# Attention scores on one core: head-pair weights 128 columns wide, 16 KB store runs, and transposes in groups of sixteen

## The chip, the cores and the metric

The kernel runs on one NeuronCore of a Trainium2 chip. A core has a matrix engine (TensorE, PE in the profile; its weight loads are listed as PEld), three engines for element-wise work (VectorE = DVE, ScalarE = ACT, GpSimd = POOL), a queue engine (SyncE = SP) that issues transfers here, and 16 DMA engines that move data between the device memory and the on-chip memory SBUF. Matmul results land in PSUM, which DVE and ACT can read[...]. The metric is the device time of one execution in microseconds (us). Before the change it is 203.78 us, the median of three runs (203.74 to 204.09).

## The reference

```python
batch, heads, seq, dim = 8, 8, 512, 64
q, k = randn(batch, heads, seq, dim), randn(batch, heads, seq, dim)   # float32
def reference(q, k):
    scale = 1.0 / np.sqrt(q.shape[-1])
    return (np.einsum('bhqd,bhkd->bhqk', q, k) * scale).astype(np.float32)
```

For each of 64 (batch, head) pairs, q (512 x 64) is multiplied with k transposed (64 x 512). The inputs are 16.8 MB, the output is 67.1 MB of float32.

## The kernel before

**Units and tiles.** The work is cut into four units `v`, each of two batches, that is 16 (batch, head) pairs. A unit gives four output tiles `t`, so there are 16 tiles `o`, each 128 partitions x 32 KB = 4 MB, covering four heads. Tiles and their stores are numbered 0 to 15 below.

**Loads and casts.** All loads are issued at the start by SP (line 78): per unit k and q, 2 MB each, into one 4 MB buffer of the pool `big`. GpSimd casts them to bf16 (line 82), in two instructions for each of k and q, into `xb`. The pool `big` has three buffers, which the loads and the output tiles share in turn: the load of unit 3 waits for the casts of unit 0, tile 0 takes the buffer whose casts (unit 1) come next, tile 1 that of unit 2, tile 2 that of unit 3, and from tile 3 on each tile waits for the store three before it.

**Transposes.** A load puts 128 rows of sequence on partitions, with two sets `s` side by side so that a 128 x 128 block holds two 64-wide heads' worth of columns. PE transposes such blocks by a product with the identity (line 107 for k, line 116 for q), eight into one PSUM tile `tp` of one bank; the pool `tpsum` has two of them. Each group of eight is then moved by four copies (line 95) of 64 partitions x 512 columns, one for each set `s` and half `h` of a head pair, into `kT` or `qz`. The four copies of a group are all on one engine; groups alternate between DVE and ACT. A unit has four groups for k and four for q. `qz` is zeroed once and holds, for each head pair, the queries of one head in the rows of that head and zeros in the others, so that a contraction over 128 rows gives a single head's scores.

**Scores.** For an output tile, eight times, four matmuls (line 126) fill a PSUM tile `ps` of two banks (three such tiles in the pool `psum`): each takes 64 weight columns of `qz` and 512 columns of `kT`, and two of them fill the upper and lower 64 partitions of one bank. Then one evacuation of 128 x 1024 float32 scales it into the tile `o`, on ACT (line 64) in turns 0, 2 and 3 of every six and on DVE (line 66) in the others. After eight evacuations SP issues the store of the 4 MB (line 141).

**The order of work.** The program order is kept on each engine. `transpose` is a generator: it yields once after the transposes of a group and once after each copy, so a group is five steps. Unit 0's groups are all run first. Then, while the tiles of unit v are computed, the steps of unit v + 1 are put between the evacuations by `take` (line 162): for v = 0 none in tile 0 and two after each evacuation from tile 1 on, later one after each evacuation and two after every fourth. Each engine works through its instructions in that order.

Of the kernel before, what the change touches and what calls it, by code (L numbers as in the profile page):

```python
# [1 line left out]

# [5 lines left out]


@with_exitstack  # L10
def kernel(
    ctx: ExitStack,
    tc: tile.TileContext,
    q: bass.AP,
    k: bass.AP,
    out: bass.AP,
):

    nc = tc.nc
    B, H, S, D = q.shape
    scale = 1.0 / (D ** 0.5)
    P = 128
    UNITS = B // 2
    N = H
    M = P // (2 * H)  # L30
    R = S // M
    J = R // 2
    RO = 16
    U = S // RO
    JJ = J // RO
    IW = 8 // JJ
    TILES = N // 2

    f32 = mybir.dt.float32
    bf16 = mybir.dt.bfloat16  # L40

    q_r = q.rearrange("(v b) g (m j) d -> v (b g m) (j d)", b=2, j=R)
    k_r = k.rearrange("(v b) g (m j) d -> v (b g m) (j d)", b=2, j=R)
    out_r = out.rearrange("(v b) (t h) (u i) k -> v (b t) (h u) (i k)", b=2, h=4, i=RO)

    consts = ctx.enter_context(tc.tile_pool(name="consts", bufs=1))

    big_pool = ctx.enter_context(tc.tile_pool(name="big", bufs=3))
    bf_pool = ctx.enter_context(tc.tile_pool(name="bf", bufs=6))
    t_pool = ctx.enter_context(tc.tile_pool(name="t", bufs=2))  # L50
    tpsum_pool = ctx.enter_context(tc.tile_pool(name="tpsum", bufs=2, space=bass.MemoryType.PSUM))
    psum_pool = ctx.enter_context(tc.tile_pool(name="psum", bufs=3, space=bass.MemoryType.PSUM))


    pinned = tc.keep_in_program_order

    n_evac = 0
    n_tp = 0

    def evacuate(dst, src):  # L60
        nonlocal n_evac

        if n_evac % 6 in (0, 2, 3):
            pinned(nc.scalar.mul(out=dst, in_=src, mul=scale))  # L64
        else:
            pinned(nc.vector.tensor_scalar(out=dst, in0=src, scalar1=scale, scalar2=None,  # L66
                                           op0=mybir.AluOpType.mult))
        n_evac += 1

    def half(h):  # L70
        return slice(h * D, (h + 1) * D)

    def load_and_cast(v):

        xf = big_pool.tile([P, 2, 2, J * D], f32, name="big")
        both = []
        for x, src in enumerate((k_r, q_r)):
            nc.sync.dma_start(out=xf[:, x], in_=src[v].rearrange("p (s c) -> p s c", s=2))
        for x in range(2):
            xb = bf_pool.tile([P, J, 2, D], bf16, name="xb")  # L80
            for s in range(2):
                pinned(nc.gpsimd.tensor_copy(out=xb[:, :, s, :],  # L82
                                             in_=xf[:, x, s].rearrange("p (j d) -> p j d", j=J)))
            both.append(xb)
        return both

    def rearrange(tp, pattern, dst):

        nonlocal n_tp
        copy = (nc.vector.tensor_copy, nc.scalar.copy)[n_tp % 2]  # L90
        n_tp += 1
        for s in range(2):
            src = tp[half(s)].rearrange(pattern, n=N, h=2)
            for h in range(2):
                pinned(copy(out=dst(s, h), in_=src[:, h]))  # L95
                yield

    def transpose(v, kb, qb):


        kT = t_pool.tile([P, N, M, 2, J], bf16, name="kT")
        qz = qzs[v % 2]
        ts[v] = (kT, qz)
        for j0 in range(0, J, 8):
            tp = tpsum_pool.tile([P, 8, P], bf16, name="tp")
            for j in range(8):
                pinned(nc.tensor.transpose(out=tp[:, j, :], identity=identity,  # L107
                                           in_=kb[:, j0 + j].rearrange("p s d -> p (s d)")))
            yield
            yield from rearrange(tp, "d j (n h m) -> d h n m j",  # L110
                                 lambda s, h: kT[half(h), :, :, s, j0:j0 + 8])
        for i0 in range(0, RO, IW):
            tp = tpsum_pool.tile([P, IW, JJ, P], bf16, name="tp")
            for i in range(IW):
                for jj in range(JJ):
                    pinned(nc.tensor.transpose(out=tp[:, i, jj, :], identity=identity,  # L116
                                               in_=qb[:, RO * jj + i0 + i].rearrange("p s d -> p (s d)")))
            yield
            yield from rearrange(tp, "d i jj (n h m) -> d h i n m jj",
                                 lambda s, h: qz[half(h), i0:i0 + IW, :, h * U:(h + 1) * U]  # L120
                                 .rearrange("d i n (m s jj) -> d s i n m jj", s=2, jj=JJ)[:, s])

    def matmul(v, t, i, x, dst):

        kT, qz = ts[v]
        pinned(nc.tensor.matmul(out=dst, lhsT=qz[:, i, 2 * t + x, :],  # L126
                                rhs=kT[:, 2 * t + x].rearrange("d m s j -> d (m s j)"),
                                start=True, stop=True))

    def scores(v, t):  # L130

        o = big_pool.tile([P, RO, S], f32, name="big")
        for i in range(0, RO, 2):
            ps = psum_pool.tile([P, 2, S], f32, name="ps")
            for w in range(2):
                for x in range(2):
                    matmul(v, t, i + w, x, ps[half(x), w, :])
            evacuate(o[:, i:i + 2, :], ps)
            yield
        src = o.rearrange("p i k -> p (i k)")  # L140
        nc.sync.dma_start(out=out_r[v, t], in_=src)  # L141

    def take(steps, count):
        for _ in range(count):
            next(steps, None)

    identity = consts.tile([P, P], dtype=bf16)
    make_identity(nc, identity)
    qzs = [consts.tile([P, RO, N, 2 * U], bf16, name=f"qz{n}") for n in range(2)]
    for qz in qzs:  # L150
        nc.vector.memset(qz, 0.0)  # L151
    cast = [load_and_cast(v) for v in range(UNITS)]

    ts = {}
    for _ in transpose(0, *cast[0]):
        pass
    for v in range(UNITS):
        ahead = transpose(v + 1, *cast[v + 1]) if v + 1 < UNITS else iter(())
        for t in range(TILES):

            for n, _ in enumerate(scores(v, t)):
                take(ahead, 1 + (n % 4 == 3) if v else 2 * (t > 0))
        for _ in ahead:
            pass


# [1 line left out]
_INS = ['q', 'k']  # L168
_OUTS = [((8, 8, 512, 512), 'float32')]


# [23 lines left out]
```

## Time and profile before

| | |
|---|---|
| median of three runs | 203.78 us |
| the profiled execution | 203.86 us |
| its span, first to last instruction | 202.1 us |
| DMA queue 1, share of 16 engines' span | 97.2% |
| bytes moved by queue 1 | 83.89 MB in 3456 packets |
| DVE, PE, ACT, POOL busy | 126.4, 107.7, 101.1, 30.5 us |
| score matmuls (line 126) | 512 of 456 ns |
| evacuations, DVE and ACT | 64 of 1221 ns, 64 of 1023 ns |
| copies of 512 columns, DVE and ACT | 64 of 687 to 688 ns, 64 of 578 ns |
| mean granted TensorE clock | 0.833 |

A row of slices cuts the span into 40 equal parts of 5.05 us; a digit is the busy share in tenths. A group's line gives line of the code, engine, operation, output <- inputs with their sizes and count, then busy time and mean duration, then the idle time of the engine before these instructions and what ended most of it. A line in time order gives start, length, engine, line, and in brackets the idle time before it and what ended it. A line of waits gives who waited for whom, with the total, the number of times and the longest. "SPq" is the queue of SP that issues transfers.

### The profile page before, as it was taken

The page shows a single profiled execution, that of the slowest core. Times are in us where ns is not written, and L with a number is a line of the kernel's source. Part 1 is how long each engine was busy: PE and PEld are TensorE (multiplying, and loading weights), DVE is VectorE, ACT ScalarE, POOL GpSimd, SP SyncE. Part 2 cuts the span into 40 slices and gives each one's busy share as a digit, 9 for nine tenths or more (in the row PEclk, how much of TensorE's full clock was granted, in tenths as well). Part 3 has the DMA queues.
Part 4 walks back from the last instruction along what each step waited for, and adds up shares of the span by engine and source line. Part 5 has one row for each costly group of instructions (what it writes and reads, how often), then busy time and mean ns, then how long its engine had stood idle before and what let it go on. Part 6 is the DMA issues. An engine that isn't in the chain of part 4 may idle for free.

```text
span 202.1 us, 1976 instructions
## 1 busy us (share of the span) xinstructions
PE 107.7 (53%) x768; PEld 55.7 (28%) x768; DVE 126.4 (63%) x130; ACT 101.1 (50%) x129; POOL 30.5 (15%) x22
## 2 busy tenths in 40 slices
PE   0033488663784767765858685856765366710000
PEld 0033344332342333332423332322322133400000
DVE  6736677974987689997569797479457064530000
ACT  2016665793639586974857566746526241520000
POOL 1277777655000000000000000000000000000000
PEclk9999999998769999997878888888589957555555
DMA  6999999999999999999999999999999999999991
GB/s 214 428 444 415 435 441 422 418 412 428 454 438 417 441 417 428 438 448 435 422 415 425 448 435 448 415 418 428 435 448 441 415 428 438 441 428 441 415 415 58
DMA packets 3464, 84.00 MB, mean 416 GB/s; under 512 B 384, under 2 KB 384, under 8 KB 384
## 3 DMA queue, kind: packets, MB, share of 16 engines
q1 hardware_dynamic: 3456, 83.89, 97.2%
q8 instruction: 6, 0.10, 0.2%
q14 instruction: 2, 0.02, 0.0%
HBM read 16.78 MB, written 67.11 MB: 415 GB/s over the span
## 4 chain that ended last, share of the span: by engine, by line
DMA 33%; DVE 14%; PE 6%; ACT 2%; issue 1%; DVEq 0%; ACTq 0%; SPq 0%
DMA out_dram<-big 33%; DVE big L66 9%; PE ps L126 6%; DVE kT L95 3%; ACT big L64 2%; DVE qz L95 1%; ACT kT L95 1%; PE tp L107 0%; DVEq L66 0%; ACTq L64 0%; SPq L141 0%
## 5 line engine op out<-in xcount | busy, mean ns | idle before, releaser
L126 PE MATMUL ps<-kT,qz 128*64 128x512 bf16 x512 | 85.0, 456 | 47.2 <-ACT big L64 36.6
L66 DVE TENSOR_SCALAR big<-ps 128x1024 f32<-128x1024 f32 x64 | 76.2, 1221 | 38.9 <-DMA out_dram<-big 25.0
L64 ACT ACTIVATE big<-ps 128x1024 f32<-128x1024 f32 x64 | 63.9, 1023 | 56.9 <-DMA out_dram<-big 24.5
L126 PEld LDWEIGHTS <-qz 128*64 128x64 bf16 x512 | 35.6, 124 | 85.9 <-issue 75.7
L82 POOL CAST xb<-big 128x2048 bf16<-128x2048 f32 x16 | 29.8, 1893 | 17.1 <-DMA big<-in_k_dram 9.6
L95 DVE COPY kT<-tp 64x512 bf16<-64x512 bf16 x32 | 22.0, 687 | 7.3 <-PE tp L107 6.9
L95 ACT COPY kT<-tp 64x512 bf16<-64x512 bf16 x32 | 18.5, 578 | 15.2 <-PE tp L107 14.9
L95 DVE COPY qz<-tp 64x512 bf16<-64x512 bf16 x32 | 22.0, 688 | 3.9 <-PE tp L116 3.3
L95 ACT COPY qz<-tp 64x512 bf16<-64x512 bf16 x32 | 18.5, 578 | 4.0 <-PE tp L116 3.6
L107 PE MATMUL tp<-identity,xb 128*128 128x128 bf16 x128 | 12.0, 253 | 15.0 <-POOL xb L82 12.4
L116 PE MATMUL tp<-identity,xb 128*128 128x128 bf16 x128 | 13.3, 272 | 7.8 <-ACT qz L95 4.1
L107 PEld LDWEIGHTS <-xb 128*128 128x128 bf16 x128 | 9.5, 114 | 20.8 <-POOL xb L82 12.4
L116 PEld LDWEIGHTS <-xb 128*128 128x128 bf16 x128 | 10.6, 123 | 14.4 <-issue 14.1
L151 DVE MEMSET qz<- 128x4096 uint32 x2 | 6.9, 3472 | 2.5 <-PEq L179 1.7
L95 ACT ACT_TABLE_LOAD x1 | 1.3, 1283 | 0.7 <-PEq L179 0.7
masks.py:199 POOL TENSOR_SCALAR_AFFINE_SELECT identity<-identity 128x128 bf16<-128x128 bf16 x1 | 0.3, 292 | 0.1
masks.py:197 POOL MEMSET identity<- 128x128 bf16 x1 | 0.2, 204 | 0.3 <-POOLq L179 0.3
L179 POOL MEMSET const-float32-0.0<- 128x1 f32 x1 | 0.1, 98 | 0.2 <-issue 0.2
L179 POOL MEMSET const-bfloat16-1.0<- 128x1 bf16 x1 | 0.1, 101 | 0.0
L179 POOL MEMSET const-uint8-127<- 128x1 uint8 x1 | 0.1, 101 | 0.0
L179 POOL MEMSET const-float32-1.0<- 128x1 f32 x1 | 0.1, 98 | 0.0
## 6 DMA issues: line engine op xcount, KB each, us to landing
out_dram<-big SPq DMA_DIRECT2D x16, 4096.0 KB, 21.2
big<-in_k_dram SPq DMA_DIRECT2D x4, 2048.0 KB, 18.9
big<-in_q_dram SPq DMA_DIRECT2D x4, 2048.0 KB, 23.9
```

What stands on the lines that cost most here:

```text
L64: pinned(nc.scalar.mul(out=dst, in_=src, mul=scale))
L66: pinned(nc.vector.tensor_scalar(out=dst, in0=src, scalar1=scale, scalar2=None, op0=mybir.AluOpType.mult))
L82: pinned(nc.gpsimd.tensor_copy(out=xb[:, :, s, :], in_=xf[:, x, s].rearrange("p (j d) -> p j d", j=J)))
L95: pinned(copy(out=dst(s, h), in_=src[:, h]))
L107: pinned(nc.tensor.transpose(out=tp[:, j, :], identity=identity, in_=kb[:, j0 + j].rearrange("p s d -> p (s d)")))
L116: pinned(nc.tensor.transpose(out=tp[:, i, jj, :], identity=identity, in_=qb[:, RO * jj + i0 + i].rearrange("p s d -> p (s d)")))
L126: pinned(nc.tensor.matmul(out=dst, lhsT=qz[:, i, 2 * t + x, :], rhs=kT[:, 2 * t + x].rearrange("d m s j -> d (m s j)"), start=True, stop=T ...
L151: nc.vector.memset(qz, 0.0)
L179: nc = _bacc.Bacc("TRN2", target_bir_lowering=False, num_devices=1)
```

## The change

Five things go together.

- An output tile covers two head pairs `x` one after the other: 8 rows per partition instead of 16 for each (`RO = 8`), so a partition of a store is two runs of 16 KB in the output, where it was one of 32 KB. The store is still 4 MB.
- A matmul takes 128 weight columns of `qz`, both heads of a pair, and fills 128 partitions of a bank; two matmuls fill a `ps` tile. The helper `matmul` goes.
- A group is 16 transposes into a PSUM tile `tp` of two banks, and its four copies have 1024 columns. A unit has two groups for k and two for q.
- The pool `tpsum` has one such tile; unit 0, whose transposes come ahead of all scores, uses the three tiles of the pool `psum` instead.
- The steps of the next unit (20, where there were 40) are spread anew: for unit 0 one after each evacuation in tile 0 and two from tile 1 on; later one after the evacuations 0, 1, 3, 5 and 7 of each tile.

```diff
-    RO = 16
+    RO = 8
     U = S // RO
     JJ = J // RO
-    IW = 8 // JJ
+    IW = 16 // JJ
...
-    out_r = out.rearrange("(v b) (t h) (u i) k -> v (b t) (h u) (i k)", b=2, h=4, i=RO)
+    out_r = out.rearrange("(v b) (t x h) (u i) k -> v (b t) (h u) x (i k)", b=2, x=2, h=2, i=RO)
...
-    tpsum_pool = ctx.enter_context(tc.tile_pool(name="tpsum", bufs=2, space=bass.MemoryType.PSUM))
+    tpsum_pool = ctx.enter_context(tc.tile_pool(name="tpsum", bufs=1, space=bass.MemoryType.PSUM))
...
-        for j0 in range(0, J, 8):
-            tp = tpsum_pool.tile([P, 8, P], bf16, name="tp")
-            for j in range(8):
+        pool, name = (tpsum_pool, "tp") if v else (psum_pool, "ps")
+        for j0 in range(0, J, 16):
+            tp = pool.tile([P, 16, P], bf16, name=name)
+            for j in range(16):
...
-                                 lambda s, h: kT[half(h), :, :, s, j0:j0 + 8])
+                                 lambda s, h: kT[half(h), :, :, s, j0:j0 + 16])
         for i0 in range(0, RO, IW):
-            tp = tpsum_pool.tile([P, IW, JJ, P], bf16, name="tp")
+            tp = pool.tile([P, IW, JJ, P], bf16, name=name)
...
-        o = big_pool.tile([P, RO, S], f32, name="big")
-        for i in range(0, RO, 2):
-            ps = psum_pool.tile([P, 2, S], f32, name="ps")
-            for w in range(2):
-                for x in range(2):
-                    matmul(v, t, i + w, x, ps[half(x), w, :])
-            evacuate(o[:, i:i + 2, :], ps)
-            yield
-        src = o.rearrange("p i k -> p (i k)")
-        nc.sync.dma_start(out=out_r[v, t], in_=src)
+        o = big_pool.tile([P, 2, RO, S], f32, name="big")
+        for x in range(2):
+            n = 2 * t + x
+            for i in range(0, RO, 2):
+                ps = psum_pool.tile([P, 2, S], f32, name="ps")
+                for w in range(2):
+                    pinned(nc.tensor.matmul(out=ps[:, w, :], lhsT=qz[:, i + w, n, :],
+                                            rhs=kT[:, n].rearrange("d m s j -> d (m s j)"),
+                                            start=True, stop=True))
+                evacuate(o[:, x, i:i + 2, :], ps)
+                yield
+        nc.sync.dma_start(out=out_r[v, t], in_=o.rearrange("p x i k -> p x (i k)"))
...
-                take(ahead, 1 + (n % 4 == 3) if v else 2 * (t > 0))
+                take(ahead, 1 + (t > 0) if v == 0 else n == 0 or n % 2)
```

In the changed kernel's lines, the k transposes are at line 109, the q transposes at 118, the copies at 95, the score matmuls at 134 and the store at 139.

## The prediction

> **What bounds the kernel now.** I read the page from the top: engines and slices, DMA queues, chain, groups, then the waits of SP's queue and the time order of the warm-up.
>
> ```profile
> span 202.1 us, 1976 instructions
> ...
> PE 107.7 (53%) x768; PEld 55.7 (28%) x768; DVE 126.4 (63%) x130; ACT 101.1 (50%) x129; POOL 30.5 (15%) x22
> ...
> DMA  6999999999999999999999999999999999999991
> ...
> q1 hardware_dynamic: 3456, 83.89, 97.2%
> ```
>
> No engine passes 63%, but the 16 DMA engines are full from the second slice to the last but one. The transfers set the time; compute matters only where a store is queued too late to find them still busy. The other 2.8% is the first packet at 1.8 us and the end.
>
> ```profile
> SPq L141 <- DVE big L66: 147.1, 16, 16.9
> ```
>
> The store queue on SP waits for the last evacuation of each tile. Each issue has a deadline: the end of the store ahead of it. These lines of the time order give it for the first stores (start us, length):
>
> ```profile
> 23.28 3.73 POOL L82 CAST xb<-big 128x2048 bf16<-128x2048 f32 x2 [1.17 <-DMA big<-in_q_dram]
> ...
> 35.05 0.35 SPq L141 DMA_DIRECT2D out_dram<-big  x1
> ...
> 44.06 0.34 SPq L141 DMA_DIRECT2D out_dram<-big  x1
> ...
> 56.91 0.33 SPq L141 DMA_DIRECT2D out_dram<-big  x1
> ```
>
> Numbering output tiles and stores from 0: in the DMA packet records the loads' last packets end at 41.9 us, store 0's at 51.6 (last engine 53.7), store 1's at 61.3 (63.3). Stores 0, 1, 2 are issued at 35.1, 44.1, 56.9: margins of 6.9, 7.6, 4.4 us. Later margins are 5 to 9 us. The first two stores are the ones that the change touches most.
>
> ```profile
> L126 PE MATMUL ps<-kT,qz 128*64 128x512 bf16 x512 | 85.0, 456 | 47.2 <-ACT big L64 36.6
> L66 DVE TENSOR_SCALAR big<-ps 128x1024 f32<-128x1024 f32 x64 | 76.2, 1221 | 38.9 <-DMA out_dram<-big 25.0
> L64 ACT ACTIVATE big<-ps 128x1024 f32<-128x1024 f32 x64 | 63.9, 1023 | 56.9 <-DMA out_dram<-big 24.5
> ...
> L95 DVE COPY kT<-tp 64x512 bf16<-64x512 bf16 x32 | 22.0, 687 | 7.3 <-PE tp L107 6.9
> L95 ACT COPY kT<-tp 64x512 bf16<-64x512 bf16 x32 | 18.5, 578 | 15.2 <-PE tp L107 14.9
> ```
>
> These are the durations that I use. Eight transposes in a row took 0.62 us with PE at full clock and 1.03 at half (51.13 us); sixteen took 1.89 at 12.4 us.
>
> [...] at 46.31 PE sat 1.6 us before a transpose until ACT's copies had emptied a tp buffer, with matmuls queued behind. [...] The granted clock fell to 0.5 at 49.4 us, after 4.7 us with 0.6 us of PE work. [...] Packet starts here stand 1.2095 us apart for 32 KB and 0.607 for 16 KB; 2 x 0.607 - 1.2095 is about 4.5 ns per extra packet.
>
> **The change, part by part.**
>
> *Wide weights.* Score matmuls go from 512 to 256, each 128 columns wide. The two 64-column halves ran side by side before (4 in 0.62 us), so PE time per evacuation stays at 0.43 us plus latency. Off the path; worth 0 here.
>
> *16 KB runs.* Each engine moves 16 packets per store where it moved 8: 8 x 4.5 ns = 0.036 us, times 16 stores = +0.6 us, on the path. Below: 0, if the cost is hidden; above: 8.5 ns, the packet's own excess over its bytes at the loads, +1.1. I take 0.6.
>
> *Fewer instructions.* In the packet records one DMA engine lags: about four fifths of its packets between 42 and 178 us take 1.24 to 1.29 us instead of 1.213, and its excess follows the matmuls finished in the packet's time (about 6 ns each). It ends last, at 200.75, against 198.9 for the next. After 42 us there are 616 matmuls; without about 240 of them it loses 1.5 us of its 4 us lag. That this is cause and not coincidence is a guess: 0 to -1.9.
>
> *Copies of 1024 columns.* No row shows 64x1024. [...] bounds are the old 0.69 and 0.58 and twice those, 1.37 and 1.16. I take 1.22 and 1.02. In all 32 x 1.22 = 39 us of DVE instead of 44: less work, in fewer but longer pieces.
>
> *One tp buffer, 16 transposes, and a schedule that starts a tile earlier.* This decides. All four copies of a group run on one engine, groups alternating between DVE and ACT. With one buffer, the next group's 16 transposes wait for the last copy of the group before, and since PE is in order every later score matmul waits too. Unit 1's four groups, which were spread over tiles 1 to 3 with two buffers, now go in tiles 0 and 1 (one step per evacuation in tile 0, two in tile 1). I walk the queues, 0.06 us per hand-over, 1.6 us per 16 transposes (between 1.07 and 1.89), 0.75 per pair of matmuls (0.43 and 0.9). The same walk with the old order gives issues at 34.7, 44.4, 57.1, 64.8 against 35.1, 44.1, 56.9, 66.2 in the trace.
>
> Unit 0 alone gains: three two-bank ps buffers let its groups overlap, done at 25.3 instead of 29.3. Tile 0's buffer still comes free only with the cast that ends at 27.0. Then on DVE four evacuations and four copies (8 x 1.22 = 9.8), with a hole of 2 while group 2's transposes wait for the fourth copy (35.0): store 0 goes at 39.5, before 41.9. Hidden, margin 2.4.
>
> Tile 1: group 2's transposes 35.0-36.6; the matmul behind them, ACT's evacuation to 38.5, two ACT copies to 40.5; tile 1's evacuation 0 to 41.5, copies three and four to 43.6. Only then group 3's transposes, to 45.2; DVE copy 46.5, evacuation 2 47.7, two copies 50.2, evacuation 3 51.4, last copy 52.6. Group 4's transposes to 54.3; matmuls of evacuation 4 to 55.0; ACT evacuation 56.1, four copies 60.2, evacuations 6 and 7 62.2. Store 1 is issued at **62.3**, where 44.1 was and the deadline is 51.6. DMA runs dry for some 10 us. All that hid these copies and transposes before was the DMA backlog, and here it is gone. Late next: nothing; store 2 follows at 68.6 against a new deadline of 73.8, and the later margins come to 4 to 11 us. (Units 2 and 3 have one group per tile, 10 steps in two tiles, with DVE at 9.8 us in every second tile, inside the period.)
>
> **The sum**, against the profiled execution (203.86 us, span 202.1, 1.8 around it; the median 203.78 is the same within the spread). Issue 62.3; first packet 1.0 later (the first load: 0.74 to 1.77); 15 stores x 9.72 (8 x 2 x 0.607 and the closing packet) = 145.9; lag of the slow engine from there, about 350 matmuls x 6.3 ns = 2.2; last packet to the end of the span 1.3 (200.75 to 202.05); outside it 1.8. Together **214.5 us**, +5.3%. The spread of 1.7 to 2 us between engines that was there at 53.7 is lost in the dry spell, which is why this is less than 203.9 + 11.6.
>
> **The rivals.**
> A, the above, 0.76: 211.8 with PE at full clock (issue 59.6), 216 at half clock (63.7); its own range 211 to 217.5.
> B, 0.09: PE stays at half clock in units 1 and 2 as well. Each group then holds PE for 1.9 us with a matmul pair at 0.86, the walk's margins for stores 8 to 11 go to nothing and DMA is dry another 3.4 us: 219. For: the page's clock row drops when PE idles. Against: PE is busy in bursts all through those units.
> C, 0.09: the long copies cost less than their columns say. At the lower bounds store 1 goes at 52.6 to 55, dry for 2 to 4.5: 204.8 to 207.5. For: longer runs at the destination. Against: kT (runs of 8) and qz (runs of 2) took the same 687 and 688 ns.
> D, the other side, 0.06: DMA is never dry. It decides where store 1 is issued before about 50.6, so the chain in tile 1 must be 12 us shorter than I walk it, which takes transposes that don't wait for the copies ahead of them. Then 203.86 + 0.6 - 1.5 = 203.0. Against it: program order on PE and one buffer. If the slow engine's lag stays too, it is 204.4.
>
> A measurement here can't tell a change below 0.2% (0.4 us) from none. Chances from the cases: faster 0.04 (most of D), same 0.02 (D and C at the edges), slower 0.94. Range 207 to 219.5: A, most of B, the top of C.
>
> **What would show it.** The DMA row has a hole at about 52 to 63 us, one or two slices of 0 to 8, and is full elsewhere; its share falls to about 93%. Store 1 is issued near 62, store 0 near 39.5. The copies show 1.22 and 1.02. PE's transposes at L109 and L118 wait for copies, up to 6 us at a time. Q1 shows 5504 packets, stores 9.72 us apart. I am wrong if store 1 goes before 52, if a second hole shows in units 1 or 2, or if 16 KB packets start more than 0.62 us apart.

## The result: 215.97 us, 5.9% slower

The changed kernel takes 215.97 us (median of 4 runs, 215.26 to 216.3) against 203.85 us; the ratio is 1.0588, 95% interval 1.056 to 1.0616. The forecast was 214.5 us, range 207 to 219.5. Its profiled execution took 216.3 us with a span of 214.5 us.

The page of the changed kernel first: the span, busy times, the DMA row in slices of 5.36 us, the queue's share, and the groups that answer to those shown of before.

```profile
span 214.5 us, 1398 instructions
...
PE 104.0 (48%) x512; PEld 49.9 (23%) x512; DVE 121.7 (57%) x98; ACT 96.3 (45%) x97; POOL 30.6 (14%) x22
...
DMA  6999999996009999999999999999999999999995
...
q1 hardware_dynamic: 5504, 83.89, 92.4%
...
L66 DVE TENSOR_SCALAR big<-ps 128x1024 f32<-128x1024 f32 x64 | 76.3, 1220 | 51.8 <-PE ps L134 30.7
L134 PE MATMUL ps<-kT,qz 128*128 128x512 bf16 x256 | 82.1, 453 | 36.8 <-ACT big L64 26.0
L64 ACT ACTIVATE big<-ps 128x1024 f32<-128x1024 f32 x64 | 63.2, 1023 | 64.7 <-PE ps L134 35.5
...
L95 DVE COPY qz<-tp 64x1024 bf16<-64x1024 bf16 x12 | 14.7, 1221 | 8.5 <-PE tp L118 8.3
...
L95 ACT COPY kT<-tp 64x1024 bf16<-64x1024 bf16 x12 | 12.1, 1005 | 7.0 <-PE tp L109 6.9
```

PE, DVE and ACT are each busy for less time than before (POOL is level), and the kernel is slower. The digits "600" are the hole: in the packet records no packet moves between 53.3 and 64.4 us. The evacuations on both engines used to wait longest for a store to land; now they wait longest for PE. In order of time, PE's transposes (L109, L118), ACT's work and SP's stores around the hole:

```profile
35.70 1.86 PE L109 MATMUL tp<-identity,xb 128*128 128x128 bf16 x16 [4.89 <-DVE kT L95]
...
40.60 0.40 SPq L139 DMA_DIRECT2D out_dram<-big  x1
...
44.51 1.87 PE L118 MATMUL tp<-identity,xb 128*128 128x128 bf16 x16 [3.93 <-ACT kT L95]
...
53.77 1.89 PE L118 MATMUL tp<-identity,xb 128*128 128x128 bf16 x16 [5.69 <-DVE qz L95]
...
56.55 1.02 ACT L64 ACTIVATE big<-ps 128x1024 f32<-128x1024 f32 x1 [11.04 <-PE ps L134]
57.47 4.05 ACT L95 COPY qz<-tp 64x1024 bf16<-64x1024 bf16 x4
61.54 4.69 ACT L64 ACTIVATE big<-ps 128x1024 f32<-128x1024 f32 x5
...
63.50 0.39 SPq L139 DMA_DIRECT2D out_dram<-big  x1
```

Three times PE stands at a group of transposes until the copies of the group before have left `tp`: 4.9, 3.9 and 5.7 us. In the kernel before, the eight groups of unit 1 wait for copies twice, 1.6 us each time; from the second to the fifth of them, up to the time of store 1 (44.1 us) and just after:

```profile
36.05 0.62 PE L107 MATMUL tp<-identity,xb 128*128 128x128 bf16 x8
...
39.81 0.62 PE L107 MATMUL tp<-identity,xb 128*128 128x128 bf16 x8
...
42.12 0.61 PE L107 MATMUL tp<-identity,xb 128*128 128x128 bf16 x8
...
46.31 0.61 PE L116 MATMUL tp<-identity,xb 128*128 128x128 bf16 x8 [1.61 <-ACT kT L95]
```

In the changed kernel ACT then waits 11.0 us for a matmul that is queued behind the third of these groups. After its one evacuation come four copies, and only then the last two evacuations of tile 1. Store 1 goes at 63.5 us; before, it went at 44.1.

**Where the 12.6 us of the last packet's end come from** (200.75 to 213.33 us). The last packet of store 0 ends at 53.30 instead of 53.65, and the packets start again at about 64.45: +11.15 - 0.35. Then 15 stores take 148.88 us to the last packet's end (64.45 to 213.33), where they took 147.10 (53.65 to 200.75): +1.78.

### The profile page after: what moved, and what is told of

Same layout as the page of the kernel before. It is cut to its first block, busy times and chain, and to the rows that moved or that the text cites. A ratio compares the mean times of both kernels' runs of the same rounds, so it can differ in the third digit from the quotient of the medians.

```text
span 214.5 us, 1398 instructions
## 1 busy us (share of the span) xinstructions
PE 104.0 (48%) x512; PEld 49.9 (23%) x512; DVE 121.7 (57%) x98; ACT 96.3 (45%) x97; POOL 30.6 (14%) x22
## 5 line engine op out<-in xcount | busy, mean ns | idle before, releaser
L134 PE MATMUL ps<-kT,qz 128*128 128x512 bf16 x256 | 82.1, 453 | 36.8 <-ACT big L64 26.0
L64 ACT ACTIVATE big<-ps 128x1024 f32<-128x1024 f32 x64 | 63.2, 1023 | 64.7 <-PE ps L134 35.5
L134 PEld LDWEIGHTS <-qz 128*128 128x128 bf16 x256 | 28.2, 113 | 84.3 <-issue 68.7
L95 DVE COPY qz<-tp 64x1024 bf16<-64x1024 bf16 x12 | 14.7, 1221 | 8.5 <-PE tp L118 8.3
L118 PE MATMUL tp<-identity,xb 128*128 128x128 bf16 x96 | 9.6, 280 | 18.9 <-DVE qz L95 11.8
L109 PEld LDWEIGHTS <-xb 128*128 128x128 bf16 x128 | 11.0, 126 | 29.2 <-issue 15.7
L118 PEld LDWEIGHTS <-xb 128*128 128x128 bf16 x128 | 11.2, 127 | 25.2 <-issue 16.4
L95 ACT COPY kT<-tp 64x1024 bf16<-64x1024 bf16 x12 | 12.1, 1005 | 7.0 <-PE tp L109 6.9
L109 PE MATMUL tp<-identity,xb 128*128 128x128 bf16 x96 | 8.4, 257 | 14.0 <-DVE kT L95 11.6
L95 DVE COPY kT<-tp 64x1024 bf16<-64x1024 bf16 x12 | 14.6, 1220 | 0.8 <-PE tp L109 0.6
L95 ACT COPY qz<-tp 64x1024 bf16<-64x1024 bf16 x12 | 12.1, 1004 | 4.5 <-PE tp L118 4.3
L109 PE MATMUL ps<-identity,xb 128*128 128x128 bf16 x32 | 3.5, 311 | 12.8 <-POOL xb L82 12.8
L95 DVE COPY kT<-ps 64x1024 bf16<-64x1024 bf16 x4 | 4.9, 1222 | 5.4 <-PE ps L109 5.3
L95 DVE COPY qz<-ps 64x1024 bf16<-64x1024 bf16 x4 | 4.9, 1222 | 0.1
L118 PE MATMUL ps<-identity,xb 128*128 128x128 bf16 x32 | 2.9, 265 | 3.1 <-ACT kT L95 1.7
```

Of the source, the lines that this page charges most:

```text
L134: pinned(nc.tensor.matmul(out=ps[:, w, :], lhsT=qz[:, i + w, n, :], rhs=kT[:, n].rearrange("d m s j -> d (m s j)"), start=True, stop=True))
```

## The experiments

All ratios are to the kernel before. "Store 1" is the time of its issue in the profiled execution; "dry" is the time in which no packet moves. Units, tiles and stores are numbered from 0.

### One half alone: wide weights and 16 KB runs

```diff
 (to the changed kernel)
-    IW = 16 // JJ
+    IW = 8 // JJ
-    tpsum_pool = ...(name="tpsum", bufs=1, ...)
+    tpsum_pool = ...(name="tpsum", bufs=2, ...)
-        pool, name = (tpsum_pool, "tp") if v else (psum_pool, "ps")
+        pool, name = tpsum_pool, "tp"          # and 8 for 16 in the loop over j0
-                take(ahead, 1 + (t > 0) if v == 0 else n == 0 or n % 2)
+                take(ahead, 1 + (n % 4 == 3) if v else 2 * (t > 0))
```

> Wide weights and 16 KB runs alone: groups of 8 transposes, two one-bank tp buffers, copies of 512 columns and the steps placed as before. Theory S (schedule and single tp buffer are the whole loss): no dry spell, stores 0 and 1 issued near 35 and 44.5 us, time 202.4 to 204.5 us, stores 9.72 us apart per engine. Rival W (16 KB writes are dearer by themselves, as the 9.83 us between stores in the changed kernel suggests): stores 9.83 us apart here too, time near 206 us.

Measured: 203.22 us (202.9 to 203.31, 7 runs), ratio 0.9969, interval 0.9958 to 0.9979. Stores 0 and 1 went at 35.0 and 44.05 us.

```profile
span 201.5 us, 1464 instructions
...
DMA  6999999999999999999999999999999999999993
...
q1 hardware_dynamic: 5504, 83.89, 98.0%
```

No hole. In the packet records an engine takes 9.719 us for a store of 16 packets through most of the run, against 9.682 for 8 packets before: 0.037 us, the 4.5 ns per extra packet of the prediction. Theory S stands, W falls. In their last two to five stores about half of the engines take 9.78 to 9.85 us, though nothing has run dry; the experiment with the dry spell comes back to this. This half of the change is a gain of 0.3%, and this kernel is the fastest of all that were run.

### The other half alone: groups of 16, one `tp`, the new placing

```diff
 (to the kernel before)
-    IW = 8 // JJ
+    IW = 16 // JJ
-    tpsum_pool = ...(name="tpsum", bufs=2, ...)
+    tpsum_pool = ...(name="tpsum", bufs=1, ...)
+        pool, name = (tpsum_pool, "tp") if v else (psum_pool, "ps")   # groups of 16 from it
-                take(ahead, 1 + (n % 4 == 3) if v else 2 * (t > 0))
+                take(ahead, 1 + (t > 0) if v == 0 else n == 0 or n % 2)
```

> The other half alone: 64-column weights and 32 KB runs as before, but groups of 16 transposes, one two-bank tp, copies of 1024 columns and the new placing of steps. Theory S: store 1 issued at 62 to 64 us, a dry spell of some 10 to 12 us, time 213 to 216 us. Rival W: the part of the loss that belongs to the runs and weights is missing, time 210 us or less. Theory L (engines that restart together run slower than engines out of step): stores after the dry spell 9.75 us apart or more, where before they were 9.68 apart; without L 9.68.

Measured: 215.89 us, ratio 1.0592 (1.0578 to 1.0607); store 1 at 63.2 us, dry from 53.3 to 64.05.

```profile
span 213.9 us, 1910 instructions
...
DMA  6999999995019999999999999999999999999993
```

The same hole, and the time of the full change within 0.1 us. So the loss is in this half. After the hole most engines take about 9.735 us per store instead of 9.682: slower, as theory L has it, though less than its 9.75.

### Two `tp` buffers

```diff
 (to the changed kernel)
-    tpsum_pool = ...(name="tpsum", bufs=1, ...)
-    psum_pool = ...(name="psum", bufs=3, ...)
+    tpsum_pool = ...(name="tpsum", bufs=2, ...)
+    psum_pool = ...(name="psum", bufs=2, ...)
```

> The changed kernel with two tp buffers of two banks and two ps buffers in place of one and three. Theory S, single buffer as the cause: transposes no longer wait for the copies just ahead of them; the walk gives store 1 at 52 to 55.5 us, a dry spell of 2 to 5 us, time 204.5 to 208 us. Rival T (the early placing of steps and the length of the copies alone, whatever the buffers): store 1 stays past 60 us, time 213 us or more.

Measured: 206.57 us, ratio 1.0133 (1.0118 to 1.0149); store 1 at 54.4 us, dry from 53.4 to 55.3.

```profile
DMA  6999999999299999999999999999999999999995
```

One buffer more takes 9.4 us of the 12.1 us away, though `ps` has one less. No transposes into `tp` wait for copies in this run; one wait of 4.2 us is left in unit 0, whose transposes go into `ps`. Theory S again; T falls.

### The copies of a group dealt to both engines

```diff
 (to the changed kernel, in rearrange)
-        copy = (nc.vector.tensor_copy, nc.scalar.copy)[n_tp % 2]
-        n_tp += 1
         for s in range(2):
             src = tp[half(s)].rearrange(pattern, n=N, h=2)
             for h in range(2):
+                copy = (nc.vector.tensor_copy, nc.scalar.copy)[n_tp % 2]
+                n_tp += 1
                 pinned(copy(out=dst(s, h), in_=src[:, h]))
```

> The changed kernel with the four copies of a group dealt to DVE and ACT in turn, so that tp is held for about 2.4 us instead of 4 to 4.9. Theory S: the walk gives store 1 at 50.5 to 53 us, at the deadline of 51.6, a dry spell of 0 to 2.5 us, time 202.5 to 205.5 us. Rival T: the same copy time in total, so store 1 past 58 us and time above 211 us.

Measured: 211.16 us, ratio 1.0345 (1.0316 to 1.0374); store 1 at 58.2 us, dry from 53.3 to 59.1. That is what rival T expected (past 58 us and above 211 us), if barely, and not what theory S did. But the run was meant to hold `tp` for about 2.4 us only, and that did not come about. The waits of this run say why:

```profile
ACT kT L95 <- DVE kT L95: 23.4, 10, 13.5
...
ACT qz L95 <- DVE qz L95: 10.8, 9, 2.2
```

(13.5 of the 23.4 us are one wait at the start of the kernel.) The copies out of one `tp` went one after the other, DVE, ACT, DVE, ACT, though they sat on two engines. For the groups of unit 1 it is 4.6 to 5.2 us from the first copy's start to the last one's end, where it is 4.1 to 7.3 in the changed kernel. So this run decides nothing between S and T. A likely reason for its gain is that evacuations could run on the engine whose copy was waiting its turn; that is not shown. It isn't the destination that orders the copies: in the kernel before, ACT and DVE copied into the same `kT` at the same time out of two `tp` buffers (38.55 to 39.24 and 38.66 to 39.82 us). That they share a PSUM tile is what is left, but it was not tried by itself.

### Steps placed later

```diff
 (to the changed kernel)
-                take(ahead, 1 + (t > 0) if v == 0 else n == 0 or n % 2)
+                take(ahead, t > 0 if v == 0 else n == 0 or n % 2)
```

> The changed kernel with one edit: no steps of unit 1 in tile 0 and one after each evacuation in tiles 1 to 3, in place of one in tile 0 and two after. Groups of 16, single tp buffer and long copies stay. If the dense placing in tiles 0 and 1 is needed for the loss, the walk gives store 1 at 48 to 49 us, in time, and store 2 at 61 to 63.5 us against a deadline of 61.4, so dry for 0.5 to 3 us, perhaps again for 1 or 2 us later: 204 to 208 us. If the single buffer alone makes the loss, whatever the placing, it stays above 213 us.

Measured: 209.3 us (208.0 to 210.75), ratio 1.029 (1.0235 to 1.0345), 1.3 us above what was expected; the profile is of the fastest of the four runs, at 208.0. Store 1 went at 47.4 us, in time; store 2 at 62.3 us, too late for the 61.3 us at which most engines were done with store 1. From 61.65 to 63.25 us most engines stood still, and again for some 1 to 1.6 us before stores 8 and 11; all 16 stood still only in the last of these spells, for 1.2 us.

```profile
DMA  6999999999988999999999989999979999999994
```

The "88", the later "8" and the "7" are these spells. The later placing alone takes 6.7 us of the 12.1 us away. In both placings that were tried with one `tp` buffer some store is late; the placing sets which one and by how much.

### Both suspects away, long copies kept

```diff
 (to the changed kernel)
     # two tp buffers, two ps buffers, as above; and
-                take(ahead, 1 + (t > 0) if v == 0 else n == 0 or n % 2)
+                take(ahead, t > 0 if v == 0 else n == 0 or n % 2)
```

> The changed kernel with two tp buffers of two banks, two ps buffers, and no steps in tile 0, one after each evacuation in tiles 1 to 3. Both suspects are taken away, groups of 16 and copies of 1024 columns stay. The walk gives stores 1 and 2 at 47.5 to 49.7 and 60 to 63 us: never dry, or dry for up to 2 us before store 2. 203 to 205.5 us. If it is the length of the copies as such that can't be hidden, 208 us or more.

Measured: 204.31 us (202.87 to 204.67, 20 runs), ratio 1.001 (0.9997 to 1.0023): no difference from before that can be measured. Stores 1 and 2 went at 46.4 and 61.35 us. The runs lie in two clusters, 202.9 to 203.7 and 204.1 to 204.7 us. The profiled one is of the upper: store 2 was some 0.9 us late for most engines.

```profile
DMA  6999999999998999999999999999999999999995
```

This kernel has the gain of the other half too, so the first experiment (203.22 us) is the nearer measure: against it the median is 1.1 us longer, and the lower cluster is about level with it. Groups of 16 and copies of 1024 columns thus cost about 1 us at most where their buffer and their place leave the stores in time, or nearly. Of the 12.1 us, the two buffers alone took 9.4 away, the placing alone 6.7, both together 11.7: neither is the whole cause, and the loss is that of the two together.

### The dry spell by itself

```diff
 (to the kernel of the first experiment, in scores)
-                evacuate(o[:, x, i:i + 2, :], ps)
+                for r in range(4 if (v, t) == (0, 1) else 1):
+                    n_evac += r > 0 and -1
+                    evacuate(o[:, x, i:i + 2, :], ps)
```

> The kernel with wide weights, 16 KB runs, groups of 8 and the steps of before, which is never dry, and one edit: each evacuation of tile 1 is done four times on its engine, with the same result, so that store 1 comes about 15 us later, near 60 us, and the DMA engines run dry for about 8 us. Theory L (engines that restart together stay in step and take longer): stores 9.80 us apart or more after the dry spell, against 9.72 without it, so 1.2 us or more on top of the dry spell, 211 to 213.5 us. Rival: the 9.83 us of the changed kernel comes from the order of its work: 9.72 apart here, 210.5 us or less.

Measured: 213.08 us, ratio 1.0451 (1.0435 to 1.0466); store 1 at 60.0 us, dry from 53.8 to 60.9, that is 7.1 us. The kernel is 9.9 us above the one without the delay, so 2.7 us more than the spell.

```profile
DMA  6999999998049999999999999999999999999995
```

In the packet records most engines take 9.835 us per store after the spell, against 9.719 without it; for 15 stores that is 1.7 of the 2.7 us, and the rest was not taken apart. Three engines that lose 1.8 us in a single store, each in the one in which a 16 KB instruction fetch falls, take 9.719 in nearly all stores after it. Theory L's forecast came true and its rival falls: a dry spell makes the later stores longer, here with the groups and the placing of the kernel before. That the engines' being in step is the reason is not shown. In the first experiment engines came to 9.78 to 9.85 us without any dry spell, with packets that started all over the 0.61 us of a packet's time, so being in step can't be the only way there.

### More matmuls, same bytes

```diff
 (to the kernel before, in scores)
                 for x in range(2):
+                    kT, qz = ts[v]
+                    pinned(nc.tensor.matmul(out=ps[half(x), w, :D], lhsT=qz[:, i + w, 2 * t + x, :],
+                                            rhs=kT[:, 2 * t + x, 0].rearrange("d s j -> d (s j)"),
+                                            start=True, stop=True))
                     matmul(v, t, i + w, x, ps[half(x), w, :])
```

> The kernel before with 512 more matmuls: ahead of each score matmul one of 64 columns into the same place, which the full one overwrites. The bytes and the order of stores stay. If the lag of the slowest DMA engine follows the number of matmuls (about 6 ns each, some 430 of them after 42 us), the last engine ends 2 to 3 us later and the time is 205.5 to 207 us. If it doesn't, 203.5 to 204.6 us.

Measured: 206.16 us, ratio 1.0117 (1.0096 to 1.0139).

```profile
DMA  6999999999999999999999999999999999999960
```

No hole anywhere in the run. In the packet records the first engine ends at the same time as before (196.85 and 196.86 us), and the last one 2.3 us later (203.05 and 200.75). One engine takes about 10.0 to 10.2 us for a store while PE works, where it took 9.8 to 10.1, and 9.68 once PE is done. With 460 more matmuls after 42 us that is 5 ns each. Each of them brings a weight load with it (in the kernel before there are 768 of each), and this run doesn't tell which of the two counts. The longer program also fetches more instructions by DMA (10 fetches of 16 KB, where there were 6). They are not the likely reason: such a fetch costs an engine about 1.3 us in a single store (seven are seen so, each on another engine than this one), while this one loses a little in every store.

## Why the prediction was right, and where its terms were off

**Which stage decides, and by what.** Right. The chain of tile 1 went as it was walked: the transposes of groups 2, 3 and 4 of unit 1 start at 35.7, 44.5 and 53.8 us (walked 35.0, 43.6 and 52.7). Two buffers alone bring back 9.4 us, the later placing alone 6.7, both together 11.7.

**Issue of store 1: 62.3 us, measured 63.5.** The term that was off is PE's pace, with the price of 16 transposes first: 1.86 to 1.91 us for each of the four groups of unit 1, not 1.6. The granted clock was 0.5 at all four (19.6 to 29.8, 33.2 to 40.0 and 43.5 to 57.1 us), and PE had idled 4.9, 3.9 and 5.7 us before groups 2 to 4. That the idling lowered the clock is the author's reading; no run shows it by itself. The bounds for half clock were the values, and the walk with them gave 63.7. Of the 1.2 us, 0.7 were there when group 2 started; from there on each group added 0.1 to 0.2.

**Copies of 1024 columns.** Right: 1.22 and 1.005 us against 1.22 and 1.02, the durations of the 1024-column evacuations in the kernel before (1221 and 1023 ns).

**First packet, end of the span, outside it.** 0.95, 1.2 and 1.8 us against 1.0, 1.3 and 1.8.

**15 stores and the slow engine: 148.1 us, measured 148.9.** The sum is near, but by luck: two of its parts were wrong and nearly made up for each other. (15 x 9.72 is 145.8, where the prediction has 145.9.) The first is "15 stores x 9.72": the price per packet is right where nothing has run dry (9.719 through most of the first experiment), but the dry spell starts all 16 engines within 0.2 us of each other, and then most take 9.835. That is 0.615 us per packet, less than the 0.62 that the prediction named as a sign of being wrong. The prediction counted the lost spread of 1.7 to 2 us only as a gain. The second is the lag of 2.2 us for the engine that follows the matmuls. Such a lag is real, as the run with more matmuls shows, but here another engine ends last. It loses 1.8 us in one store late in the run (11.68 us, to 174.5), takes 9.719 from then on, and finishes 1.3 us after the middle one. In that store falls a 16 KB instruction fetch, from 170.75 us on: this engine starts no store packet between 170.03 and 171.62 us, and its packets around this gap take 0.73 to 1.08 us instead of 0.61. The fetches at 81.2 and 125.3 us each leave such a gap on one engine too. The prediction had no term for them.

**Wide weights at 0, runs at +0.6, fewer matmuls at -1.5.** Together -0.9; the first experiment shows -0.6 (203.22 to 203.80). Of the parts, the runs are shown at +0.6 (16 x 0.037). That leaves -1.2 for the fewer matmuls, against -1.5, but no run shows it by itself. The last engine of that run ends 0.5 us sooner than before.

**The rivals.** B, half clock in units 1 and 2 with further spells, did not come in the changed kernel: of the eight groups of units 2 and 3, five took 1.05 us, at a granted clock of 1.0. Further spells did come with the later placing; their cause was not looked into. C falls with the copies' durations. D, never dry, is what the first experiment is, at 203.2 us against the 203.0 worked out for it; it needed groups of 8, the two buffers and the old placing.

## What to carry to other kernels

Where the DMA queue is always full (97.2% of the span before), each store has a deadline, and a change of schedule is priced by the store that misses it, not by busy time: here PE, DVE and ACT all had less to do and the kernel lost 12 us in one place. Twice the group in one buffer instead of two is the same memory, but it ties the matrix engine, in program order, to the last copy of every group: here PE stood 4.9, 3.9 and 5.7 us for it in unit 1. A dry spell also costs after it ends: here 0.116 us in each of the 15 stores that followed, for most engines.

## What was not expected of the hardware

- Most of the 16 DMA engines, once they had run dry and restarted together, moved the same store in 9.835 us instead of 9.719 (16 KB packets), or about 9.735 instead of 9.682 (32 KB), nearly to the end of the run. Why is open.
- With 460 more matmuls, each with its weight load, while stores were written, one DMA engine ended 2.3 us later, some 5 ns for each, with the first engine unmoved (196.85 and 196.86 us).
- A 16 KB instruction fetch held up the stores of one DMA engine for 1.3 us (before) to 1.9 us (in the changed kernel), and there it made that engine the last.
- Two matmuls with 128 weight columns filled a `ps` tile in 0.59 us, four with 64 columns in 0.62; in a row, four of the first took 1.02 us and eight of the second 1.05: the halves had already run side by side.
- Copies out of one PSUM tile on ACT and DVE ran one after the other: 4.6 to 5.2 us for two of 1.2 us and two of 1.0. Whether the hardware asks for this or only the waits in the program do is not shown.
